# A column mean over 8192 rows: from VectorE accumulation to fp32 matmuls on four TensorE column tiles

## The chip, the cores and the metric

The kernel runs on one core of a Trainium2 chip. A core has TensorE (matrix products, results in the PSUM memory), VectorE (elementwise work), ScalarE, GpSimd, a SyncE that here only issues transfers, and 16 DMA engines that carry data between HBM, the large memory outside the core, and SBUF, the working memory of 128 partitions. The metric is the device time of one execution in microseconds (us), the median of several runs.

## The reference

The input is one matrix of 8192 x 8192 fp32 numbers, 268.4 MB. The output is the mean of each column, 8192 numbers.

```python
def setup_inputs():
    return {"x": np.random.randn(8192, 8192).astype(np.float32)}

def reference(x):
    return np.mean(x, axis=0)
```

Each input number is used once, in one addition.

## The kernel before

The matrix is cut into 64 row tiles of 128 rows, one row per partition, and each row tile into four column blocks of 2048 columns. One load brings 128 x 2048 numbers, 1 MB, in which each partition gets a contiguous run of 8 KB. VectorE adds each loaded tile to one of four accumulators in SBUF. What is left at the end is a sum over 128 partitions, and that is done by matmuls with a stationary column of ones, which hold 1/8192.

```python
    CB = 2048
    n_cb = (N + CB - 1) // CB                 # 4 column blocks
    n_rt = (M + P - 1) // P                   # 64 row tiles
    FREE = nc.PSUM_BANK_SIZE_BYTES // 4       # 512
    # pools: ld bufs=8, acc bufs=1, sg bufs=1, psum bufs=4, res bufs=2
        ones = sg.tile([P, 1], mybir.dt.float32)
        nc.any.memset(ones[:], 1.0 / M)
        accs = [accp.tile([P, CB], mybir.dt.float32, name=f"acc{i}") for i in range(n_cb)]
        # ... the first row tile is loaded into firsts ...
        for ri in range(1, n_rt):
            r0 = ri * P
            for cb in range(n_cb):
                c0 = cb * CB
                t = ld.tile([P, CB], mybir.dt.float32)
                nc.sync.dma_start(out=t[:], in_=x[r0:r0 + P, c0:c0 + CB])      # L42
                # ... ri == 1 adds firsts[cb] and t (L44) ...
                    nc.vector.tensor_add(out=accs[cb][:], in0=accs[cb][:], in1=t[:])  # L46
        for cb in range(n_cb):
            c0 = cb * CB
            r = resp.tile([1, CB], mybir.dt.float32)
            for fi in range(0, CB, FREE):
                ps = psp.tile([1, FREE], mybir.dt.float32)
                nc.tensor.matmul(out=ps[:], lhsT=ones[:], rhs=accs[cb][:, fi:fi + FREE])  # L52
                nc.vector.tensor_copy(out=r[:, fi:fi + FREE], in_=ps[:])       # L53
            nc.sync.dma_start(out=out[c0:c0 + CB], in_=r[:1, :])               # L54
```

Of the kernel before, what the change touches and what calls it, by code (L numbers as in the profile page):

```python
# [1 line left out]

# [4 lines left out]


@with_exitstack
def kernel(  # L10
    ctx: ExitStack,
    tc: tile.TileContext,
    x: bass.AP,
    out: bass.AP,
):
    nc = tc.nc
    M, N = x.shape
    P = nc.NUM_PARTITIONS
    CB = 2048
    n_cb = (N + CB - 1) // CB  # L20
    n_rt = (M + P - 1) // P
    FREE = nc.PSUM_BANK_SIZE_BYTES // 4

    with tc.tile_pool(name="ld", bufs=8) as ld, \
         tc.tile_pool(name="acc", bufs=1) as accp, \
         tc.tile_pool(name="sg", bufs=1) as sg, \
         tc.tile_pool(name="psum", bufs=4, space=bass.MemoryType.PSUM) as psp, \
         tc.tile_pool(name="res", bufs=2) as resp:
        ones = sg.tile([P, 1], mybir.dt.float32)
        nc.any.memset(ones[:], 1.0 / M)  # L30
        accs = [accp.tile([P, CB], mybir.dt.float32, name=f"acc{i}") for i in range(n_cb)]
        firsts = []
        for cb in range(n_cb):
            t0 = ld.tile([P, CB], mybir.dt.float32)
            nc.sync.dma_start(out=t0[:], in_=x[0:P, cb * CB:(cb + 1) * CB])  # L35
            firsts.append(t0)
        for ri in range(1, n_rt):
            r0 = ri * P
            for cb in range(n_cb):
                c0 = cb * CB  # L40
                t = ld.tile([P, CB], mybir.dt.float32)
                nc.sync.dma_start(out=t[:], in_=x[r0:r0 + P, c0:c0 + CB])  # L42
                if ri == 1:
                    nc.vector.tensor_add(out=accs[cb][:], in0=firsts[cb][:], in1=t[:])  # L44
                else:
                    nc.vector.tensor_add(out=accs[cb][:], in0=accs[cb][:], in1=t[:])  # L46
        for cb in range(n_cb):
            c0 = cb * CB
            r = resp.tile([1, CB], mybir.dt.float32)
            for fi in range(0, CB, FREE):  # L50
                ps = psp.tile([1, FREE], mybir.dt.float32)
                nc.tensor.matmul(out=ps[:], lhsT=ones[:], rhs=accs[cb][:, fi:fi + FREE])  # L52
                nc.vector.tensor_copy(out=r[:, fi:fi + FREE], in_=ps[:])  # L53
            nc.sync.dma_start(out=out[c0:c0 + CB], in_=r[:1, :])  # L54


# [1 line left out]
_INS = ['x']  # L58
_OUTS = [((8192,), 'float32')]


# [23 lines left out]
```

## Time and profile before

| What | Value |
|---|---|
| time, median of 3 runs | 659.93 us (659.87 to 660.07) |
| profiled span | 658.1 us |
| VectorE busy | 587.1 us, 89% of the span |
| TensorE busy | 17.0 us, 3% |
| read from HBM | 268.44 MB, 408 GB/s over the span |
| one 1 MB load, from issue to landing (median) | 17.5 us |

How to read the profile: the page divides the span into 40 equal slices of 16.5 us and gives for each engine a digit, the busy share in tenths. A group of instructions is listed by its source line, with its count, its busy time, the mean duration of one in ns, and after the bar the idle time of its engine just before it and what ended that time (the releaser). "L46" is the line that is marked in the code above. A load is issued by SyncE, waits in a queue with the loads ahead of it, and lands when its last byte is there; up to eight are under way, so the time from issue to landing is far longer than the transfer of one. PEld rows are the loads of TensorE's stationary operand.

### The profile page before, as it was taken

Reading aid. Unit: us, or ns where it says so; the run is one execution under the profiler, and the core shown is the slowest. Engines: PE = TensorE matmul, PEld = TensorE weight load, DVE = VectorE, ACT = ScalarE, POOL = GpSimd, SP = SyncE. Lnnn points to the kernel's source line nnn. Section 1 sums busy time; section 2 is a strip of 40 time slices with the busy share of each in tenths; the row PEclk is TensorE's granted clock in tenths of the full one; section 3 lists DMA queues with packets and bytes.
Section 4 is the critical chain, followed back from the end, with each engine's and each line's share of the span. In section 5 each row is a group of like instructions: output and inputs, shape, how many; then the busy total and the mean of one; then the engine's idle time right before and its main releaser. Section 6 shows DMA issues by size and latency. Waiting matters only on the chain.

```text
span 658.1 us, 1142 instructions
## 1 busy us (share of the span) xinstructions
PE 17.0 (3%) x32; PEld 2.8 (0%) x32; DVE 587.1 (89%) x268; POOL 0.3 (0%) x5
## 2 busy tenths in 40 slices
PE   0000000000000000000000000000000000000028
PEld 0000000000000000000000000000000000000001
DVE  0999989999999998999999999899999999899997
POOL 0000000000000000000000000000000000000000
PEclk9999999999999999999999999999999999999999
DMA  8999999999999999999999999999999999999980
GB/s 366 422 422 422 422 421 421 421 423 421 422 422 422 422 421 421 421 422 422 422 422 422 422 422 422 419 422 421 421 422 422 422 422 422 421 421 421 422 349 2
DMA packets 36880, 268.55 MB, mean 408 GB/s; under 512 B 4100, under 2 KB 4100, under 8 KB 4100
## 3 DMA queue, kind: packets, MB, share of 16 engines
q1 hardware_dynamic: 36872, 268.48, 98.1%
q14 instruction: 8, 0.07, 0.0%
HBM read 268.44 MB, written 0.03 MB: 408 GB/s over the span
## 4 chain that ended last, share of the span: by engine, by line
DMA 85%; DVE 12%; PE 1%; issue 1%; SPq 0%; DVEq 0%
DMA t<-in_x_dram 85%; DVE acc L46 12%; PE ps L52 1%; DVE acc L44 0%; DVE r L53 0%; SPq L35 0%; DVEq L46 0%; SPq L42 0%; DVEq L44 0%
## 5 line engine op out<-in xcount | busy, mean ns | idle before, releaser
L46 DVE TENSOR_TENSOR acc<-acc,t 128x2048 f32<-128x2048 f32 x248 | 568.0, 2292 | 51.4 <-DMA t<-in_x_dram 51.4
L52 PE MATMUL ps<-acc,ones 128*1 128x512 f32 x32 | 17.0, 691 | 638.0 <-DVE acc L46 637.9
L44 DVE TENSOR_TENSOR acc<-t,t 128x2048 f32<-128x2048 f32 x4 | 9.2, 2292 | 16.1 <-DMA t<-in_x_dram 16.1
L53 DVE COPY r<-ps 1x512 f32<-1x512 f32 x16 | 10.3, 673 | 1.0 <-PE ps L52 0.9
L52 PEld LDWEIGHTS ps<-acc,ones 128*1 128x1 f32 x32 | 2.8, 91 | 651.2 <-issue 646.5
L69 POOL MEMSET const-bfloat16-1.0<- 128x1 bf16 x1 | 0.1, 101 | 0.0
L69 POOL MEMSET const-uint8-127<- 128x1 uint8 x1 | 0.1, 101 | 0.0
L30 POOL MEMSET ones<- 128x1 f32 x1 | 0.1, 98 | 0.3 <-POOLq L69 0.3
L69 POOL MEMSET const-float32-0.0<- 128x1 f32 x1 | 0.1, 98 | 0.2 <-issue 0.2
L69 POOL MEMSET const-float32-1.0<- 128x1 f32 x1 | 0.1, 98 | 0.0
## 6 DMA issues: line engine op xcount, KB each, us to landing
t<-in_x_dram SPq DMA_DIRECT2D x256, 1024.0 KB, 17.5
out_dram<-r SPq DMA_DIRECT2D x4, 8.0 KB
```

What stands on the lines that cost most here:

```text
L30: nc.any.memset(ones[:], 1.0 / M)
L44: nc.vector.tensor_add(out=accs[cb][:], in0=firsts[cb][:], in1=t[:])
L46: nc.vector.tensor_add(out=accs[cb][:], in0=accs[cb][:], in1=t[:])
L52: nc.tensor.matmul(out=ps[:], lhsT=ones[:], rhs=accs[cb][:, fi:fi + FREE])
L53: nc.vector.tensor_copy(out=r[:, fi:fi + FREE], in_=ps[:])
L69: nc = _bacc.Bacc("TRN2", target_bir_lowering=False, num_devices=1)
```

## The change

The running sums move from VectorE to TensorE. Every row tile is multiplied from the left with ones (holding 1/8192), and the products accumulate in PSUM over all 64 row tiles, so that the sum over partitions and the sum over row tiles are one operation. The 16 column groups of 512 columns are spread over four PSUM banks and, within a bank, over the four 32-column tiles of TensorE's array: group (b, q) goes to bank b, partitions 32q to 32q+31. The stationary operand is 128 x 32, so that all 32 partitions of a group hold the same sum. The purpose of the column tiles is that matmuls on different tiles can run at the same time.

The loads become 4 MB each, a whole row tile with 32 KB per partition, in five buffers. The last row tile comes in pieces, three of 1 MB (one bank each) and four of 256 KB, so that little work is left after the last byte. Each bank is copied to SBUF as a whole, and one row of every 32 is written out, by ScalarE's queue.

```diff
-    CB = 2048
-    n_cb = (N + CB - 1) // CB
-    n_rt = (M + P - 1) // P
-    FREE = nc.PSUM_BANK_SIZE_BYTES // 4
+    F = 512
+    NB = N // (4 * F)
+    n_rt = M // P
+    SPL = 128
... the pools, the accumulators and the two loops of before are removed ...
+    ld = ctx.enter_context(tc.tile_pool(name="ld", bufs=5))
... pools lastp, sg, psum and res, with bufs=1 each ...
+    ones = sg.tile([P, 32], f32)
+    nc.vector.memset(ones[:], 1.0 / M)
+    banks = [psp.tile([P, F], f32, name=f"bank{b}") for b in range(NB)]
+
+    def mm(b, q, c0, w, rhs, start, stop):
+        nc.tensor.matmul(
+            out=banks[b][32 * q:32 * q + 32, c0:c0 + w],
+            lhsT=ones[:],
+            rhs=rhs,
+            start=start,
+            stop=stop,
+            tile_position=(0, 32 * q),
+            skip_group_check=True,
+        )
+
+    for ri in range(n_rt - 1):
+        t = ld.tile([P, N], f32)
+        nc.sync.dma_start(out=t[:], in_=x[ri * P:(ri + 1) * P, :])
+        for b in range(NB):
+            for q in range(4):
+                c = (b * 4 + q) * F
+                mm(b, q, 0, F, t[:, c:c + F], ri == 0, False)
+
+    r0 = (n_rt - 1) * P
+    out_v = out.rearrange("(b q c) -> b q c", b=NB, q=4)
+    x_v = x.rearrange("r (b q c) -> r b q c", b=NB, q=4)
+    for b in range(NB - 1):
+        t = lastp.tile([P, 4, F], f32, name=f"last{b}")
+        nc.sync.dma_start(out=t[:], in_=x_v[r0:r0 + P, b])
+        for q in range(4):
+            mm(b, q, 0, F, t[:, q, :], False, True)
+        r = resp.tile([P, F], f32, name=f"r{b}")
+        nc.vector.tensor_copy(out=r[:], in_=banks[b][:])
+        nc.scalar.dma_start(out=out_v[b], in_=r[0:128:32, :])
+    b = NB - 1
+    r = resp.tile([P, F], f32, name=f"r{b}")
+    for s in range(F // SPL):
+        t = lastp.tile([P, 4, SPL], f32, name=f"lasts{s}")
+        nc.sync.dma_start(out=t[:], in_=x_v[r0:r0 + P, b, :, s * SPL:(s + 1) * SPL])
+        for q in range(4):
+            mm(b, q, s * SPL, SPL, t[:, q, :], False, s == F // SPL - 1)
+    nc.vector.tensor_copy(out=r[:], in_=banks[b][:])
+    nc.scalar.dma_start(out=out_v[b], in_=r[0:128:32, :])
```

More of the change, by code (lines that the diff above doesn't have):

```diff
@@ L16 @@
     nc = tc.nc
+    f32 = mybir.dt.float32
     M, N = x.shape
     P = nc.NUM_PARTITIONS
-    CB = 2048
-    n_cb = (N + CB - 1) // CB
-    n_rt = (M + P - 1) // P
-    FREE = nc.PSUM_BANK_SIZE_BYTES // 4
[L24 to L54, printed above, removed]
@@ new lines @@
+    F = 512
[3 more added lines that the diff above has]
+    ld = ctx.enter_context(tc.tile_pool(name="ld", bufs=5))
+    lastp = ctx.enter_context(tc.tile_pool(name="lastp", bufs=1))
+    sg = ctx.enter_context(tc.tile_pool(name="sg", bufs=1))
+    psp = ctx.enter_context(tc.tile_pool(name="psum", bufs=1, space=bass.MemoryType.PSUM))
+    resp = ctx.enter_context(tc.tile_pool(name="res", bufs=1))
+    ones = sg.tile([P, 32], f32)
+    nc.vector.memset(ones[:], 1.0 / M)
+    banks = [psp.tile([P, F], f32, name=f"bank{b}") for b in range(NB)]
```

## The prediction

> **What bounds the kernel now.** I read four views, in this order: the 40 slices with the DMA rows, to see what is busy all the time; the waits, to see who waits for whom; a table of stretches, to see where the transfers begin and stop; and the timeline and the chain of waits at the end.
>
> ```profile
> DVE  0999989999999998999999999899999999899997
> DMA  8999999999999999999999999999999999999980
> GB/s 366 422 422 422 422 421 421 421 423 421 422 422 422 422 421 421 421 422 422 422 422 422 422 422 422 419 422 421 421 422 422 422 422 422 421 421 421 422 349 2
> q1 hardware_dynamic: 36872, 268.48, 98.1%
> ...
> L46 DVE TENSOR_TENSOR acc<-acc,t 128x2048 f32<-128x2048 f32 x248 | 568.0, 2292 | 51.4 <-DMA t<-in_x_dram 51.4
> ```
>
> Two rows look full, VectorE and the DMA. The group of adds tells which of them leads: one add takes 2292 ns, a load of 1 MB at 422 GB/s takes 1.0486 MB / 422 GB/s = 2.485 us, and before the 248 adds VectorE stood idle for 51.4 us, all of it waiting for loads. So the transfers set the pace and VectorE follows with some 8% to spare. All DMA engines are busy in 98.1% of the span: no wait is left between transfers that a better schedule could remove.
>
> ```profile
> 3.50:15.50 12.00, 0.00 (x0) 0.00 (x0) 0.00 (x0) 0.00 (x0) 1.00 1.01 426
> 20.00:620.00 600.00, 0.00 (x0) 0.00 (x0) 549.72 (x241) 0.00 (x0) 1.00 1.01 422
> 636.00:638.00 2.00, 0.14 (x1) 0.11 (x2) 1.80 (x2) 0.00 (x0) 1.00 1.00 418
> 638.00:642.00 4.00, 4.00 (x5) 0.50 (x4) 4.00 (x3) 0.00 (x0) 1.00 0.21 86
> 643.00:656.00 13.00, 11.84 (x27) 1.99 (x25) 11.65 (x16) 0.00 (x0) 1.00 0.00 2
> ```
>
> The columns are the stretch, its length, the busy time of TensorE, its weight loads, VectorE and GpSimd, the clock, the DMA share and the GB/s. Data flow from about 3.2 us; most engines are done at 638.4 us and a straggler finishes near 642. The last load was issued at 625.3 us and took 17.4 us to land, so at 642.7. From there to the end of the span, 658.1, are 15.4 us in which nothing is fetched. Note also that the 12 us before the first add ran at 426 GB/s and everything later at 422.
>
> ```profile
> 640.72 2.27 DVE L46 TENSOR_TENSOR acc<-acc,t 128x2048 f32<-128x2048 f32 x1
> 641.23 0.13 PEld L52 LDWEIGHTS ps<-acc,ones 128*1 128x1 f32 x1 [0.73 <-issue]
> 642.08 0.13 PEld L52 LDWEIGHTS ps<-acc,ones 128*1 128x1 f32 x1 [0.73 <-issue]
> ...
> 644.12 2.27 DVE L46 TENSOR_TENSOR acc<-acc,t 128x2048 f32<-128x2048 f32 x1
> 644.22 0.08 PEld L52 LDWEIGHTS ps<-acc,ones 128*1 128x1 f32 x1 [0.34 <-issue]
> 644.65 0.08 PEld L52 LDWEIGHTS ps<-acc,ones 128*1 128x1 f32 x1 [0.34 <-issue]
> ...
> 654.97 0.68 DVE L53 COPY r<-ps 1x512 f32<-1x512 f32 x1 [0.18 <-PE ps L52]
> ```
>
> This is the tail. The last add cannot start at 642.7, since copies of earlier column blocks hold VectorE; it runs from 644.12 to 646.39. Then TensorE has work left until 654.95, the last copy runs to 655.65, and the output's way to memory ends the span at 658.11. The weight loads are the clock of TensorE: one fp32 matmul is two records with one weight load each, 0.855 us apart at first and 0.428 us apart from 643.8 on, after some 6 us of unbroken work. A warm fp32 matmul over 512 columns thus costs 2 x 0.428 = 0.856 us.
>
> **What the Trainium skill says.** "FP8 and Floating Point Precision", section TensorE Precision Notes: true fp32 is four passes through the array. The trace agrees: 0.856 us is four times 512 columns at 2.4 columns per ns, 0.853 us. "TensorE: Matmul & The Clock Gate", Part 3, Packing small matmuls: matmuls on different column tiles run at the same time in one array; three column tiles gave 2.38 times at M = 32 and N = 512, and matmuls start and end in program order. No run so far shows tiles, or this with fp32. The same page, Part 1: the array starts at half clock and reaches full clock after some 3.4 us of work. The trace agrees in kind (0.855, then 0.428 us), with a longer cold time. "DMA: Bandwidth & Descriptors", section Why small descriptors are slow: each packet costs a few cycles beside its bytes. The trace fits: its packets are 8192 bytes, and their records are 309 ns nearly throughout before the first add (8192 / 0.309 = 26.5 GB/s, times 16 engines 424 GB/s), and 313.8 ns on average later.
>
> **The change part by part.** *Removed: all adds and the accumulators.* 252 adds x 2.292 us = 577 us of VectorE. It lies beside the transfers and is worth nothing by itself, but its last 2.27 us and the delay before it lie in the tail.
>
> *Added: TensorE work per row tile.* 16 fp32 matmuls over 512 columns, each two records. With no overlap: 16 x 0.856 = 13.7 us per row tile. A row tile's 4.194 MB take 4.194 / 0.424 = 9.9 us to arrive. So TensorE must overlap at least 1.38 times, or it becomes the bound. In program order each tile's two records follow each other, and the next matmul is on the next tile. Records of one tile cannot run together, so if starts are in order, the second record of one tile pairs with the first of the next: 0.428 us per matmul, 16 x 0.428 = 6.9 us per row tile. That fits in 9.9 with 3 us of pause. I take this case. If all four tiles ran abreast it would be 3.4 us, with the same end, since TensorE waits for data either way. If TensorE falls back to its cold rate, the pairs need 13.7 us per row tile, it then has no pause, and the trace shows it warm after 6 us of that; so I charge nothing for the clock.
>
> *Moved: the loads.* The 256 loads of 1 MB with 8 KB rows become 63 of 4 MB with 32 KB rows, and 7 small ones. Two things can speed them up. First, if the adds are what lifts a packet from 309 to 313.8 ns, their removal returns 268.4 MB / 422 - 268.4 / 427 = 636.1 - 628.6 = 7.5 us at most; matmuls read the same memory, so I count half, -3.5 us. Second, if a packet grows with the row to 32 KB, the overhead over a pure 32 bytes per cycle falls: 8192 bytes at the skill page's fabric rate of 435 GB/s take 301 ns, against 309, so 8 ns per packet; with one in place of four packets 3 x 8 ns per 32 KB are saved. Per engine that is 512 rows x 24 ns = 12 us, an estimate from that page's rate. Whether packets grow I cannot tell from the trace, where the row is itself 8 KB; I give it a half, -6 us.
>
> *Last row tile.* Three pieces keep 8 KB rows. The last MB comes as four pieces with 512-byte runs, 2048 runs in all, 128 for each engine. At 16 cycles of data plus the same 8 ns of overhead, 19 + 8 = 27 ns, it takes 3.5 us in place of 2.5: +1 us.
>
> *The tail.* After the last 256 KB: four matmuls over 128 columns, whose records are a quarter of 0.428, so 0.107 us, five to eight of them in sequence, 0.5 to 0.9 us; one copy of a bank, 128x512, like the present copy of 512 columns, 0.67 us; then from the copy's end to the span's end 658.11 - 655.65 = 2.46 us as now; some 0.2 us for waits. Sum 4.1 us against 15.4: -11.3 us. The straggler of 4 us I leave as it is.
>
> Sum: 659.9 - 11.3 + 1 - 3.5 - 6 = 640.1 us.
>
> **The rivals.** *TensorE becomes the bound.* If fp32 on column tiles does not overlap, 64 x 13.7 = 877 us, plus 13 us until the first 4 MB is there and 5 at the end: near 895. If it overlaps a little, say 0.7 us per matmul, 64 x 11.2 + 18 = 735. For it: nothing here shows overlap, weight loads in the same rows may hold up the neighbour tile, and each matmul needs two of them. Against it: the weight loads of the present kernel hide entirely under the running matmul (0.34 us idle and 0.08 us load in a beat of 0.428), the skill page has measured 2.38 times, and 1.38 are enough. I give it 17%.
>
> *The transfers gain nothing, and only the tail is won.* If matmul reads slow the packets as adds do and packets stay at 8 KB, the sum is 659.9 - 11.3 + 1 = 649.6, 1.6% faster. If the 512-byte pieces cost more than reckoned, or the straggler grows since few large loads leave less slack, 652. For it: 98.1% is full already and the bytes are the same. Against it: 426 against 422 GB/s before the first add. I give it about a fifth, and the cases near it count as within 2%.
>
> *Both transfer gains come in full.* 649.6 - 7.5 - 12 = 630.
>
> **Range and chances.** With TensorE not the bound (83%) the time lies between 630 and 652 with its middle near 640; the line for 2% is 646.7. About three quarters of this mass is below it: 0.62 faster, 0.21 within 2%, and 0.17 slower, which is the rival of TensorE alone. The predicted time is 640 us and the range 629 to 656; what lies outside is nearly all far above it.
>
> **What the profile would show.** If the steps are right: DMA again 9 in all slices, at 424 GB/s or more; TensorE idle before most row tiles, its releaser the load; per row tile a burst of about 7 us; four to five us from the last load's landing to the end. Packets: about 36,000 if they stay at 8 KB, near 11,000 if they grow. Wrong would be a TensorE row of 9 with the DMA row at 7 or less and the load queue waiting on TensorE (no overlap); a DMA rate that stays at 422 with VectorE idle (the adds did not slow the packets); a last MB that takes 5 us or more; or a straggler of 10 us after the other engines are done.

## The result, and the profile after

The changed kernel takes 634.38 us, median of 4 runs (634.25 to 634.66), against 659.97 us before; the ratio is 0.961 (95% interval 0.960 to 0.963). It is 3.9% faster, 25.6 us. The prediction was 640 us, 629 to 656.

First the page of the changed kernel: busy rows in 40 slices, the DMA rows, and the two largest groups. L43 is the matmul in the helper `mm`.

```profile
PE   1564754656547546565476554655646646556466
DVE  0000000000000000000000000000000000000001
PEclk9868668667786686677866778668766686687767
DMA  9999999999999999999999999999999999999996
GB/s 371 433 440 437 432 431 431 428 431 430 431 433 430 431 430 433 431 432 431 430 431 431 428 434 430 431 431 430 433 428 431 431 430 431 432 435 430 431 427 233
DMA packets 11665, 268.74 MB, mean 425 GB/s; under 512 B 1136, under 2 KB 3184, under 8 KB 3200
...
L43 PE MATMUL bank<-t,ones 128*32 128x512 f32 x2016 | 359.8, 880 | 265.1 <-DMA t<-in_x_dram 265.1
L43 PEld LDWEIGHTS bank<-t,ones 128*32 128x32 f32 x2016 | 81.2, 153 | 542.5 <-DMA t<-in_x_dram 310.8
```

The DMA row is still the full one, so the bound is the same as before. What changed is its rate, 431 GB/s where it was 422, and the number of packets, 11,665 where it was 36,880: the packets grew with the row, to 32 KB. VectorE is empty. TensorE is busy somewhat over half the time, and the idle time before this group, 265.1 us, ends with a load throughout. Two stretches give the rates in numbers (stretch, length, busy times of TensorE, weight loads, VectorE and GpSimd, clock, DMA share, GB/s):

```profile
3.50:15.50 12.00, 2.36 (x12) 0.68 (x16) 0.00 (x0) 0.00 (x0) 1.00 1.01 437
20.00:600.00 580.00, 336.57 (x1896) 76.08 (x1900) 0.00 (x0) 0.00 (x0) 0.74 1.00 431
```

The mean clock of TensorE is 0.74 of full speed: with pauses of some 4 us before each row tile, part of most bursts runs at the half-speed beat. In a run below the pauses are 1.1 us and the clock is 1.00.

The timeline of one row tile shows how the matmuls run. Each line is a start, a duration, and a number of records; "x4" counts the weight loads that start together, and the "x8" are those of the first two beats.

```profile
82.41 0.20 PEld L43 LDWEIGHTS bank<-t,ones 128*32 128x32 f32 x8 [4.40 <-DMA t<-in_x_dram]
82.42 6.58 PE L43 MATMUL bank<-t,ones 128*32 128x512 f32 x32 [3.40 <-DMA t<-in_x_dram]
83.27 0.20 PEld L43 LDWEIGHTS bank<-t,ones 128*32 128x32 f32 x4 [0.66 <-issue]
84.13 0.20 PEld L43 LDWEIGHTS bank<-t,ones 128*32 128x32 f32 x4 [0.66 <-issue]
84.98 0.20 PEld L43 LDWEIGHTS bank<-t,ones 128*32 128x32 f32 x4 [0.66 <-issue]
```

Four records start in each beat of 0.855 us, as many as there are column tiles (with a single tile, below, it is one per beat). This burst is at the cold rate: 32 records in 8 beats, 6.6 us. The first burst of the kernel goes from the cold beat to one of 0.43 us within itself and takes 5.4 us.

Last the end of the chain of waits: start, duration, what.

```profile
618.32 3.74 SPq L76
622.06 0.04 issue
622.10 6.68 DMA lasts<-in_x_dram
628.78 0.04 issue
628.83 0.47 PE bank L43 x8
629.30 0.02 issue
629.32 0.69 DVE r L79
```

The last piece lands at 628.78 us, 13.9 us earlier than the last load before (642.7), and 3.8 us later the span ends at 632.6, where it was 15.4. The gain, 25.5 us of the span, therefore splits into two: 13.9 in the transfers and 11.6 in the tail.

### The profile page after: what moved, and what is told of

Its sections match the earlier page's. It is cut to its first block, busy times and chain, and to the rows that moved or that the text cites. A ratio compares the mean times of both kernels' runs of the same rounds, so it can differ in the third digit from the quotient of the medians.

```text
span 632.6 us, 4331 instructions
## 1 busy us (share of the span) xinstructions
PE 363.6 (57%) x2072; PEld 82.7 (13%) x2072; DVE 2.9 (0%) x5; POOL 0.2 (0%) x4
## 2 busy tenths in 40 slices
DMA packets 11665, 268.74 MB, mean 425 GB/s; under 512 B 1136, under 2 KB 3184, under 8 KB 3200
## 4 chain that ended last, share of the span: by engine, by line
DMA 87%; PE 11%; SPq 1%; issue 0%; DVE 0%
DMA t<-in_x_dram 86%; PE bank L43 11%; DMA lasts<-in_x_dram 1%; SPq L76 1%; SPq L55 0%; DVE r L79 0%
## 5 line engine op out<-in xcount | busy, mean ns | idle before, releaser
L43 PE MATMUL bank<-t,ones 128*32 128x512 f32 x2016 | 359.8, 880 | 265.1 <-DMA t<-in_x_dram 265.1
L43 PEld LDWEIGHTS bank<-t,ones 128*32 128x32 f32 x2016 | 81.2, 153 | 542.5 <-DMA t<-in_x_dram 310.8
L70 DVE COPY r<-bank 128x512 f32<-128x512 f32 x3 | 2.1, 692 | 625.3 <-PE bank L43 625.3
L43 PE MATMUL bank<-last,ones 128*32 128x512 f32 x24 | 2.7, 592 | 0.0
L43 PE MATMUL bank<-lasts,ones 128*32 128x128 f32 x32 | 1.5, 279 | 0.5 <-DMA lasts<-in_x_dram 0.5
L43 PEld LDWEIGHTS bank<-last,ones 128*32 128x32 f32 x24 | 0.7, 110 | 2.2 <-issue 1.9
L43 PEld LDWEIGHTS bank<-lasts,ones 128*32 128x32 f32 x32 | 0.8, 109 | 1.6 <-DMA lasts<-in_x_dram 1.3
L79 DVE COPY r<-bank 128x512 f32<-128x512 f32 x1 | 0.7, 692 | 1.1 <-PE bank L43 1.1
```

The costliest lines, as they stand in the source:

```text
L43: nc.tensor.matmul(out=banks[b][32 * q:32 * q + 32, c0:c0 + w], lhsT=ones[:], rhs=rhs, start=start, stop=stop, tile_position=(0, 32 * q), ...
L70: nc.vector.tensor_copy(out=r[:], in_=banks[b][:])
L79: nc.vector.tensor_copy(out=r[:], in_=banks[b][:])
```

## The experiments

The kernel before, on the same chip beside each group of runs, took 659.90 to 660.04 us (medians).

### Large packets, few transfers, or the absence of adds: four runs

Between 422 and 431 GB/s three things changed at once. The first run goes back to 1 MB loads and keeps the matmuls.

```diff
-        t = ld.tile([P, N], f32)
-        nc.sync.dma_start(out=t[:], in_=x[ri * P:(ri + 1) * P, :])
         for b in range(NB):
+            t = ld.tile([P, 4 * F], f32)          # bufs=20
+            nc.sync.dma_start(out=t[:], in_=x[ri * P:(ri + 1) * P, b * 4 * F:(b + 1) * 4 * F])
... the matmuls read the same columns from the four smaller tiles
```

> The matmuls stay; the loads are 1 MB with 8 KB rows again, 20 buffers. Packet size (own theory): packets are 8192 bytes again, near 309 ns, so 64 x 32 packets per engine cost about 5 ns more per 8 KB, 2048 x 5.7 = 12 us more: 646 us, DMA rate 424 to 427 GB/s. Removal of the adds (rival): what was slow was the adds beside the transfers, so the rate stays at 431 and the time near 634. Matmuls slow the packets as the adds did (second rival): 314 ns per packet, 422 GB/s, 652 us.

Measured: 648.71 us, ratio 0.983 (0.982 to 0.985), 14.3 us more than the changed kernel. The same stretches of its trace:

```profile
3.50:15.50 12.00, 6.64 (x32) 0.79 (x32) 0.00 (x0) 0.00 (x0) 0.89 1.01 427
20.00:600.00 580.00, 377.86 (x1856) 43.02 (x1856) 0.00 (x0) 0.00 (x0) 0.69 1.01 421
```

No VectorE at all, and yet 427 GB/s in the first 12 us and 421 afterwards, as in the kernel before. So the fall from 426 to 422, from which the prediction had read a cost of the adds, comes without them too. The changed kernel has it as well, 437 against 431; what makes the first microseconds faster is not known. The time lies between the 646 us of the packet size and the 652 us of matmuls that slow the packets as adds would. The other runs decide between these.

The second run keeps 63 loads of 4 MB but breaks the landing place into runs of 8 KB.

```diff
-        t = ld.tile([P, N], f32)
-        nc.sync.dma_start(out=t[:], in_=x[ri * P:(ri + 1) * P, :])
+        t = ld.tile([P, 4, 4 * F + 16], f32)
+        nc.sync.dma_start(out=t[:, :, 0:4 * F], in_=x[ri * P:(ri + 1) * P, :].rearrange("r (b c) -> r b c", b=NB))
... the matmuls read the same columns from t[:, b, :]
```

> The same 63 loads of 4 MB, but each partition's 32 KB land in four runs of 8 KB with 64 bytes between them, so that no run in SBUF is longer than 8 KB. Packet size (own theory): some 36,000 packets of 8192 bytes and the same time as with 1 MB loads, about 646 us. Number of transfers (rival): it was the 256 loads with their completions that cost time, so 4 MB loads keep the gain whatever the packet: 634 to 637 us.

Measured: 644.66 us, ratio 0.977 (0.975 to 0.978).

```profile
DMA packets 35857, 268.74 MB, mean 418 GB/s; under 512 B 1136, under 2 KB 3184, under 8 KB 3200
...
20.00:600.00 580.00, 326.85 (x1864) 73.75 (x1868) 0.00 (x0) 0.00 (x0) 0.76 1.01 425
```

With everything else equal, packets of 8 KB in place of 32 KB cost 644.66 - 634.38 = 10.3 us. The mean records agree in sign: 312.0 ns for 8 KB, so 1248 for four, against 1219 ns for 32 KB. Over the 504 packets of one engine these 29 ns would be 14.6 us, more than the time shows. And 252 loads in place of 63, with packets equal, cost 648.71 - 644.66 = 4.1 us, some 21 ns a load. Both theories hold, with 10 and 4 us. Why more loads cost this, completions or a queue that holds fewer bytes (eight loads of 1 MB against five of 4 MB), was not told apart. The records show two traces of it: each further load brings 16 packets of 4 bytes (4,161 packets under 512 B in the first run, 1,136 in this one), some 1.9 us per engine, and the 8 KB records are 2.0 ns longer (314.0 against 312.0 ns), some 4.0 us per engine.

The third run puts the adds back beside the changed kernel, on tiles of their own.

```diff
+    da = sg.tile([P, 2048], f32)
+    db = sg.tile([P, 2048], f32)                  # both set to 0.0; ld bufs=4
     for ri in range(n_rt - 1):
+        for _ in range(4):
+            nc.vector.tensor_add(out=da[:], in0=da[:], in1=db[:])
```

> The changed kernel with 252 VectorE adds of 128x2048 on two tiles of their own, which nothing waits for, beside the transfers (and four load buffers in place of five, for room). If adds slow the packets (rival): mean record of a 32 KB packet 15 to 20 ns longer than 1219 ns, 512 x 15 to 20 = 8 to 10 us more: 642 to 645 us. If packet size alone made the difference (own theory): 634 to 635 us and 431 GB/s.

Measured: 634.23 us, ratio 0.961 (0.960 to 0.963).

```profile
20.00:600.00 580.00, 337.73 (x1896) 75.88 (x1900) 563.15 (x246) 0.00 (x0) 0.74 1.00 431
```

VectorE is busy for 563 of 580 us and the rate is 431 as without it. Adds beside matmuls cost these transfers nothing. This agrees with the Trainium skill, "SBUF — State Buffer", section SBUF: two separate sides, by which engines and DMA reach this memory through ports of their own; the prediction had read the trace against it.

The fourth run gives the kernel before the large loads, adds and all.

```diff
-                t = ld.tile([P, CB], mybir.dt.float32)
-                nc.sync.dma_start(out=t[:], in_=x[r0:r0 + P, c0:c0 + CB])
+            t = ld.tile([P, N], mybir.dt.float32)      # bufs=4, one load per row tile
+            nc.sync.dma_start(out=t[:], in_=x[r0:r0 + P, :])
...
-                    nc.vector.tensor_add(out=accs[cb][:], in0=accs[cb][:], in1=t[:])
+                    nc.vector.tensor_add(out=accs[cb][:], in0=accs[cb][:], in1=t[:, c0:c0 + CB])
```

> The kernel before, adds and all, with 4 MB loads of 32 KB rows (four buffers), each added in four parts. Packet size (own theory): near 11,000 packets, 430 GB/s, the last load lands some 12 us earlier, near 631 us in the span; the tail is longer, since four adds (9.2 us) and 16 matmuls follow the last landing: first add 2.3, matmuls 14 to 16, copy 0.7, output 2.5, so 21 us: near 653 us in all. If the gain in the transfers needs the adds to be gone (rival): rate 422, last landing at 643 or later, 664 us or more.

Measured: 651.72 us, ratio 0.988 (0.986 to 0.989). A stretch of its trace and the end of its chain of waits:

```profile
20.00:600.00 580.00, 0.00 (x0) 0.00 (x0) 527.13 (x238) 0.00 (x0) 1.00 1.00 432
...
626.87 8.90 DVE acc L45 x4
635.77 0.60 DVE r L52
636.41 10.47 PE ps L51 x24
646.91 0.68 DVE r L52
```

With adds alone on the loaded tiles the rate is 432 GB/s, with matmuls alone it was 431, with both 431: neither slows the packets by an amount that shows. The last load has landed at 626.87 us at the latest, some 16 us earlier than before, so the gain in the transfers is there to have without TensorE. But 8.3 us of it show: four adds now follow the last landing, then the matmuls, and the tail is 650.1 - 626.9 = 23.2 us. Large loads pay in the transfers and are paid for in the tail, which is why the change cuts the last row tile up.

### Is it the column tiles that keep TensorE under the transfers? Two runs

> Only the order of the 16 matmuls of a row tile is changed: the four banks of one column tile in a row, then the next column tile, so that neighbours in program order are on the same tile and only the 4 changes of tile can overlap. Own theory (overlap of column tiles is what keeps TensorE under the transfers): 28 to 32 of 32 records one after the other, 12.0 to 13.7 us per row tile, 785 to 895 us, with the load queue waiting on TensorE and the DMA share near 0.75. Rival (an fp32 matmul with 32 columns is simply faster, and the tiles play no part): bursts and time as in the changed kernel, 634 us.

```diff
-        for b in range(NB):
-            for q in range(4):
+        for q in range(4):
+            for b in range(NB):
```

Measured: 635.64 us in one run, much less than my theory asked for. The waits that ended idle time of TensorE (us in total, times, longest), the long stretch, and the timeline at the end ("last" and "lasts" are the pieces of the last row tile and come in program order after all of "t", "lasts" after all of "last"):

```profile
PE bank L43 <- DMA t<-in_x_dram: 67.3, 61, 13.1
20.00:600.00 580.00, 527.47 (x1907) 142.24 (x1903) 0.00 (x0) 0.00 (x0) 1.00 1.00 431
```

```profile
626.11 0.61 PE L43 MATMUL bank<-last,ones 128*32 128x512 f32 x3
626.51 0.59 PE L43 MATMUL bank<-t,ones 128*32 128x512 f32 x1
626.54 1.85 PE L43 MATMUL bank<-last,ones 128*32 128x512 f32 x12
627.83 0.39 PE L43 MATMUL bank<-lasts,ones 128*32 128x128 f32 x6
628.23 1.02 PE L43 MATMUL bank<-last,ones 128*32 128x512 f32 x2
628.66 0.42 PE L43 MATMUL bank<-lasts,ones 128*32 128x128 f32 x6
629.09 0.59 PE L43 MATMUL bank<-last,ones 128*32 128x512 f32 x1
```

A burst took 8.87 us here, 20.7 beats of 0.428 us for 32 records, still under the 9.7 us of a load. The timeline shows how: a record of "t" starts at 626.51 after three of "last", two of "last" start at 628.23 after six of "lasts", and one more at 629.09. What is left of "t" at that time belongs to the fourth column tile, the last in this order, and the three "last" records that start together are as many as there are other tiles. TensorE here starts matmuls on a free column tile ahead of earlier ones that wait for a busy tile. So neighbours need not alternate, if other tiles' work comes soon after. The rate stays at 431 GB/s with TensorE busy for 527 of 580 us in place of 337. The run did not remove the overlap, only worsened it; the next one does.

```diff
-            out=banks[b][32 * q:32 * q + 32, c0:c0 + w],
+            out=banks[b][0:32, c0:c0 + w],
...
-            tile_position=(0, 32 * q),
+            tile_position=(0, 0),
```

The start flag is set for q = 0 alone, and rows 0, 8, 16 and 24 of the one group are written out, so separate sums of the four column groups are left out.

> All matmuls go to the first column tile; the four column groups of a bank are summed into the same 32 partitions, so the output is not the column mean (one group's sums are not kept apart from another's), but the loads, the number and size of matmuls and the tail are the same. Own theory (only matmuls on different column tiles run together, and the order within a row tile does not matter much because TensorE takes them out of order): 32 records of 0.428 us one after the other, 13.7 us per row tile, near 895 us, load queue waiting on TensorE. Rival (neighbouring fp32 records overlap whatever the tile, or the 32-column form is cheaper): under 700 us.

Measured: 899.92 us in one run.

```profile
DMA  9999886777877867887879788778777787685000
...
L43 PE MATMUL bank<-t,ones 128*32 128x512 f32 x2016 | 867.8, 593 | 13.2 <-DMA t<-in_x_dram 13.2
```

```profile
SPq L55 <- PE bank L43: 772.5, 58, 16.4
```

TensorE never waits after the first load, and the load queue waits 772.5 us for it. 867.8 us for 2016 records are 0.430 us each, 13.8 us per row tile. The column tiles are therefore what keeps fp32 matmuls under the transfers: 8 beats per row tile against 32, which at 0.43 us a beat is 3.4 us against 13.8, a factor of four where 1.38 were needed. In the changed kernel's trace the bursts are partly at the half-speed beat and take 4.9 to 6.6 us.

### What the pieces at the end are worth: four runs

> The last row tile is one 4 MB load like the others. The last byte then lands near 626 us in the span (all at 431 GB/s), and 16 matmuls follow it: 3.4 us warm to 6.8 us cold, then the copy 0.7 and the output 2.6. Theory that the pieces shorten the tail: 636 to 638 us. Rival (the pieces cost in the transfers about what they save in the tail, since the GB/s fall below 350 in the last 10 us): 633 to 635 us.

```diff
-    for ri in range(n_rt - 1):
+    for ri in range(n_rt):
... the pieces are removed; the four copies and outputs follow the loop
```

Measured: 639.32 us, ratio 0.968 (0.967 to 0.970), 4.9 us more than with pieces.

```profile
622.00:624.00 2.00, 2.00 (x12) 0.39 (x8) 0.00 (x0) 0.00 (x0) 0.53 0.96 401
624.00:625.00 1.00, 0.64 (x8) 0.00 (x0) 0.00 (x0) 0.00 (x0) 1.00 0.46 197
625.00:626.00 1.00, 0.00 (x0) 0.00 (x0) 0.00 (x0) 0.00 (x0) 1.00 0.38 164
626.00:627.00 1.00, 0.00 (x0) 0.00 (x0) 0.00 (x0) 0.00 (x0) 1.00 0.31 131
```

```profile
627.87 0.04 issue
627.92 5.04 PE bank L43 x32
```

(This trace is of the fastest execution, 638.21 us.) Most engines are done at 624 us; 197, 164 and 131 GB/s are seven to five engines of 26.9 GB/s each, which finish near 627, and the landing is at 627.87. The same straggling was in the kernel before (638.4 to 642.7). After it come 16 matmuls, which start at the cold beat after a wait of 3.3 us: 5.04 us in place of 0.47.

In the next run the pieces have 1 KB runs (`SPL = 256`).

> The last MB comes in two pieces of 512 KB with 1 KB runs in place of four with 512-byte runs. In the changed kernel the last of the four was issued only at 622.1 us, after a wait for an earlier transfer of the same completion semaphore; with two fewer transfers that wait falls on loads that landed long before. If late issue and short runs hold up the end: last landing at 626 to 627 us, 632 to 633 us. If the end is set by the bytes and a straggling engine: 634 us.

Measured: 634.15 us, ratio 0.961 (0.959 to 0.963), with the landing at 628.34 us: the second case. In the next one the outputs are one transfer:

```diff
-        nc.scalar.dma_start(out=out_v[b], in_=r[0:128:32, :])     # per bank
+    nc.scalar.dma_start(out=out_v, in_=r[0:128:32, :, :])         # once, after the last copy
```

> Four pieces with 512-byte runs as in the changed kernel, but the four outputs are one transfer at the very end. That leaves the semaphores of the three early outputs to the loads, so the last piece waits for a load that landed near 609 us and not for one of the last. If late issue holds up the end: last landing at 626 to 627 us, 632 to 633 us. If it is the 512-byte runs: as in the changed kernel, 634 us.

Measured: 635.00 us, ratio 0.962 (0.961 to 0.964), slightly worse than the changed kernel. The chain of waits shows that the last piece is issued at the same time as before:

```profile
589.24 17.61 SPq L74
606.84 0.04 issue
606.89 15.23 SPq L74
622.11 0.04 issue
622.16 6.70 DMA lasts<-in_x_dram
```

The issue instructions themselves take 17.6 and 15.2 us, which would fit a queue that has no room while 4 MB loads stand in it; what they wait for the trace does not name. The semaphore theory fell. In the last run of the four the last MB is whole (`SPL = 512`).

> The last MB comes as one load with 8 KB rows like the other three of the last row tile. If what holds up the end is a few straggling engines, the landing stays near 628 us, and only the four matmuls of 512 columns in place of 128 are added after it (one beat of two records, 0.9 to 1.7 us in place of 0.5): 634.5 to 635.5 us. If the short runs cost time, the landing moves to 626 us: 633 us or less.

Measured: 634.48 us, ratio 0.962 (0.960 to 0.963), landing at 628.16 us. So landing (628.2 to 628.9) and time (634.15 to 635.00) hardly depend on how the last MB is cut; that short runs and late issue hide behind the stragglers would fit this, and was not tested by itself. What counts is that the last row tile comes in pieces of 1 MB: four of them do as well as three and four small ones.

### Larger packets still

```diff
+    for ri in range(0, n_rt - 1, 2):               # 31 loads of 8 MB, one of 4 MB; bufs=2, SPL = 256
+        n = 2 if ri < n_rt - 2 else 1
+        t = ld.tile([P, 2, N], f32, name="t")
+        nc.sync.dma_start(out=t[:, 0:n, :], in_=x[ri * P:(ri + n) * P, :].rearrange("(p r) c -> p r c", r=n))
... 16 matmuls for each of the n rows per partition
```

> 8 MB loads of two rows per partition, 64 KB in one run, in two buffers; last MB in two pieces of 1 KB runs (which alone gave 634.15). If packets keep growing to 64 KB: half of the overhead left in a 32 KB packet is saved, 8 ns of 1219 per 32 KB less by half, 512 x 4 ns = 2 us, and 32 transfers fewer at some 20 ns, 0.7 us: 631 to 632 us. If packets stop at 32 KB: 633.5 to 634 us. If two buffers are too few (a load can be issued only when TensorE is done with the one before): gaps in the DMA row, 640 us or more.

Measured: 631.69 us, ratio 0.957 (0.956 to 0.959), the fastest of all.

```profile
DMA packets 6144, 268.73 MB, mean 427 GB/s; under 512 B 608, under 2 KB 1632, under 8 KB 1648
20.00:600.00 580.00, 275.53 (x1920) 67.17 (x1920) 0.00 (x0) 0.00 (x0) 0.73 1.00 432
```

The packets grew to 64 KB, 2426 ns on average, 1213 per 32 KB. Two buffers were enough. The last landing came at 625.99 us. Against the run with the same last pieces (634.15 us) the gain is 2.5 us; the run also has 31 fewer large loads, and what of the gain is theirs was not told apart.

## Why the prediction was right, point by point

- **What bounds the kernel** held: the DMA row is full before and after, and TensorE waits for loads.
- **The tail** held: 4.1 us were predicted from the last landing to the end, 3.8 measured; -11.6 us in place of -11.3. The run with 1 MB loads, whose transfers are those of the kernel before, gains 11.3 us, the tail alone.
- **The straggler** stayed as it was left: 3.9 us from the bulk's end to the landing without pieces, 4.3 before.
- **Packets that grow with the row** was right in mechanism and halved for doubt. The estimate of 12 us stood for certain growth, the sum took 6, and the measured term is 10.3.
- **The adds slow the packets** was wrong: -3.5 us in the sum, 0.15 us between the run with the adds back and the changed kernel, which is within their spread. The 426 against 422 GB/s of the kernel before are found in the same way without adds, and so are its 8 KB records of 309.7 ns at first and 313.8 later (309.5 and 313.8 in the run with 1 MB loads).
- **The number of loads** was missing from the sum: -4.1 us. It takes the place of the adds in explaining the last GB/s.
- **The 512-byte pieces**, +1 us in the sum, measured nothing: the cuts of the last MB lie within 0.9 us of each other.
- **TensorE** was right in its result, and wrong in two steps. "If starts are in order, the second record of one tile pairs with the first of the next", 6.9 us per row tile: in fact starts are not in order between tiles, all four run abreast, and 8 beats are 3.4 us warm. And "if TensorE falls back to its cold rate, the pairs need 13.7 us": it does fall back around its pauses, and a cold burst of four abreast is 6.6 us, which happens to be near the number predicted for another reason. The rival without overlap was put at 895 us and measured at 899.9. That an fp32 matmul is four passes through the array no run here shows; the traces show two records of 0.428 us each.

With the measured terms the sum is 659.9 - 11.6 - 10.3 - 4.1 = 633.9 us against 634.4; with the predicted ones it was 640.1. The errors of 4.3 us in the packets, 4.1 in the loads and 1 in the pieces pull one way and the 3.5 for the adds the other, which with the 0.3 of the tail makes the 6.2 us between 640.1 and 633.9. That the prediction came near is thus partly an error that offset others.

## What to carry to other kernels

When the DMA row is full and the bytes cannot be fewer, look at the packets: a contiguous run of 32 KB per partition in place of 8 KB was worth 10.3 us here, 1.6%, and large loads reached the same rate whichever engine did the sums. Large loads lengthen what follows the last landing, so cut up the last one only. A difference in rate between two stretches of a trace names no cause by itself: everything that differs between them is a candidate.

## What was not expected of the hardware

- Matmuls on different column tiles of TensorE start out of program order. The Trainium skill, "TensorE: Matmul & The Clock Gate", Part 3, The mechanism, says that matmuls start and end in program order; in the run with one tile's matmuls in a row, records of a later piece started up to 1.26 us before an earlier one (627.83 against 629.09 us), so here the measurement decides.
- The fp32 factor of four column tiles is four: 8 beats of 0.43 us against 32 for the same 16 matmuls.
- Packets follow the run length up to 64 KB: 312 ns for 8 KB, 1219 for 32 KB, 2426 for 64 KB. From the last two, 1207 ns per further 32 KB and some 12 ns fixed per packet, an estimate from two points.
